# Other places for the steps of two kinds of attention heads in a hand-written instruction order

## The chip, the cores and the metric

The kernel runs on one core of a Trainium2 chip. The time is the device time of one execution in microseconds (us), the median of several runs. A core has a matrix engine (TensorE; PE for its products and PEld for its weight loads in the profile), a vector engine (VectorE, DVE), a scalar engine (ScalarE, ACT), GpSimd (POOL) and SyncE (SP); SP and POOL issue the DMAs here. Each engine works off its own instructions in the order in which the program gives them, and waits on semaphores for the others.

## The reference, cut to what matters

One layer over x (1024 positions by 2048), in fp32. Two groups of eight heads each, of 128 columns, come out of one projection:

```python
hn = rmsnorm(h, norm_mix_g)
sb_q, sb_k, sb_v, sb_g, df_q, df_k, df_v, df_g = split(hn @ w_in)
# stick-breaking heads: weight of key s for query t > s
z = q @ k.T / sqrt(128)
w = exp(log_sigmoid(z[t, s]) - sum(softplus(z[t, j]) for s < j < t))
sb_out = w @ v
# differential heads: two halves of 64 columns, partial rope on q and k
a = softmax(s1) - lam * softmax(s2)            # causal
df_out = rmsnorm(a @ v, subln_g)
mixed = concat(sb_out * silu(sb_g), df_out * silu(df_g))
h = h + mixed @ w_out
h = h + sigmoid(rmsnorm(h) @ w_ple_gate) * (p @ w_ple_proj)
out = rmsnorm(h)
```

## The kernel before, in words

**Arithmetic.** Every fp32 operand of the matrix engine is split into a high and a low part (hi by a cast on ACT, lo by a subtraction on DVE), and a product is three matmuls: hi by hi, hi by lo, lo by hi. So each operand costs ACT a pass and DVE a pass before PE can use it.

**Stages, by the trace.** Up to about 636 us the V and gate columns of the projection are made for all heads and stored (`vg_d`). From there to about 1080 us the heads of the first half of the positions run (`half == 1` in the code, 512 keys), then to about 1640 us those of the second half (`half == 0`, 1024 keys: the new 512 and those of the first half, kept as k_d, kl_d and v_d). The last pair's attention, 1640 to 1766 us, runs beside the first products of the output projection (class `Seven`, operands named A11, A12, S2, S4, S1, S3, A22). Then come the output projection, the gate of the embedding, and the last norm.

**Order of the heads.** `ORDER` alternates a differential head (DF) and a stick-breaking head (SB): a pair. A pair takes 57.4 us in the first half and 74 us in the second.

**The ticks.** `unit` multiplies one head's q and k columns: four chunks of weights, two accumulators (q and k, PSUM tag "acc"), four blocks each, so 32 ticks a head. A tick is three matmuls (L252, L253, L254) and then a call of `side.tick()`. `Side` is a queue of steps with a due tick. A step added with offset t runs floor(t) + 1 ticks later, and among steps of one tick the smaller number goes first; a step with a negative offset runs at once. Offsets are counted from the end of the head's own unit, those of `taken` and of the last pair's operands from the start of one. A step's own parts come by `side.later(dt, ...)`, floor(dt) ticks on (0: in the same tick). The attention of a pair thus lies between the projection matmuls of the heads behind it. The orders of PE, DVE and ACT are the order in which the steps run; those of SP and POOL are made by a scheduler, so a load can go out ahead when its buffer is free. All offsets are in the table `TICK` (L42 to L56).

**The steps.**
- Weights of the projection (`wprep`): raw load, high part on ACT (`whi`, L173), low part on DVE (`wlo`, L169) in the first half; in the second half the low part is loaded back from memory (L175).
- `taken` (L1400, L1404 for SB): the accumulators leave PSUM. For DF (L1426) it goes on by `q_turn` and `k_turn`, seven and eight offsets counted from `taken`: shuffle, product with sine, product with cosine, sum (the rope, four DVE passes, L1452 to L1455); the high parts on ACT (L1432, L1436); the low parts of the two halves on DVE (q L1441, k L1443); and for k the ends, four short casts on ACT (L1450). The store of k for the second half goes out on POOL behind its low parts.
- `scores` (L333 to L336) puts z for one block of 128 rows into one of two z buffers. For SB, `sb_scores` are the offsets of the four row blocks, and `sb_stick` those of the mask (L346), the sigmoids (L359, L360), the scan (L366) and the product (L370) behind it. For DF there are two z per row block; `df_soft` are the offsets, counted from z, of the maximum (`top`, L383), of the exponential (L391, counted from the maximum), of the reciprocal, lambda and scaling (L396 to L398), and of the combination of both softmaxes (L403).
- `values`: V is turned (L418) and split (L420, L423); `sb_v`, `df_v`.
- `turn` (L438): blocks of weights are transposed into PSUM tag "t" (two buffers for turned weights, products and msq); `parts` takes them out: `lead` and `awh` on ACT (L456, L457), `lead` and `awl` on DVE (L461, L462). `mix` (L480 to L485) multiplies by V. `sb_turn` and `df_turn` are the offsets of the second pair of row blocks in each half.
- `sums`: copy (L496) and sum (L499, with a product L501 for SB) of the mixed blocks. `squared` and `norm` for DF: square, product with the gain (L513), split, two matmuls with ones (msq, L530 and L531), two roots on ACT (L534, L535), and four DVE passes (L538 to L541).
- `df_vg`, `sb_vg`: load of V and gate, two products with the norm (L1386), the sigmoid (L1389), the product (L1392).
- Two table loads on ACT per pair (L224 in the profile), for logarithm and exponential (`LOGS`) and for sigmoids (`SIGS`).
- Last pair (`operands`): two offsets for each of the four blocks of an operand, its load (SP) and its split (ACT L627, DVE L633); `wf` the loads of the first output weights, `begun` their splits.

Of the kernel before, what the change touches and what calls it, by code (L numbers as in the profile page):

```python
# [39 lines left out]
GVT = 1, 2, 3, 4, 5, 6, 7, 8, 14, 15, 16, 17  # L40
GLAT = {'S4': 4, 'S1': 4, 'S2': 4}
TICK = {  # L42
    "turn": 76, "lag": 15, "gap": (4, 6), "parts": (1, 2), "vparts": (1, 2), "sums": (1, 2), "squared": (3, 5), "norm": (1, 4),
    "df_scores": (-20, -16, -12, -8, -4, 0, 4, 8), "df_turn": (17, 17), "df_v": -4, "df_norm": 44.5,
    "sb_scores": (-2, 6, 14, 22), "sb_turn": (32, 36), "sb_v": 23,
    "df_soft": (1, 1.5, 4, 5.5), "sb_stick": (1, 1, 3, 5.5), "taken": (28, 31), "sb_split": (1, 2), "kv": 9,
    "df_vg": (24, 36, 37, 57, 58.5), "sb_vg": (6, 17, 18, 26, 27.5),
    "q_turn": (1.5, 5, 7, 8.5, 12, 14, 15.5), "k_turn": (1.5, 13, 14.5, 16, 19.5, 21, 22, 23.5),
# [5 lines left out]
    "begun": (86.5, 92.5, 93.5, 94.5, 92.5),  # L54
}
LAM0 = 0.8 - 0.6 * math.exp(0.0)  # L56
NEG = -1.0e30
# [2274 lines left out]
```

## Time and profile before

| | |
|---|---|
| median of the runs | 2399.39 us (2396.4, 2399.39, 2399.98) |
| the profiled execution | 2398.69 us, its span in the trace 2396.9 us |
| mean granted clock | 0.996 of full speed |
| weights, bytes moved | 359.16 MB read, 203.69 MB written, 235 GB/s |

The span is the time between the first and the last instruction of the trace; the execution's own time is 1.8 us longer. Of the busy shares (the page's first part) it is to be kept in mind that matmuls follow each other before the earlier one has ended, so a busy PE can still lose time between two starts. In lines of the timeline the first number is the start, the second the duration, and the bracket at the end is the idle time of that engine before the instruction, with the one that ended it. In the table of stretches the columns are the busy time and number of instructions of PE, PEld, DVE, ACT and POOL, the granted clock, the DMA's share, and GB/s.

### The profile page before, as it was taken

The numbers are of one execution on the slowest core, as the hardware profiler recorded it, in microseconds if no ns is written. First come the engines' busy times: TensorE is split into PE (matmuls) and PEld (weight loads), VectorE is DVE, ScalarE is ACT, GpSimd is POOL, SyncE is SP. The second block draws the span as 40 slices with busy tenths as digits, with TensorE's granted clock in tenths as the row PEclk, the third lists the DMA queues.
The fourth block names the chain that finished last, engine by engine and source line by source line (L and its number), as shares of the span: only waits on it lengthen the run. The fifth ranks groups of instructions, "written<-read, shape, count | busy, mean of one in ns | idle before, by whom it ended". The sixth has DMA issues, their size and how long they took to land.

```text
span 2396.9 us, 32668 instructions
## 1 busy us (share of the span) xinstructions
PE 2333.0 (97%) x11110; PEld 1934.2 (81%) x11110; DVE 1791.2 (75%) x3115; ACT 1273.9 (53%) x2305; POOL 296.7 (12%) x439
## 2 busy tenths in 40 slices
PE   9999999999999999998999999999899999999998
PEld 7878878888788888877888888887778887888787
DVE  6487786665678888877777777777687987687687
ACT  6323253333366666667666666666542444532455
POOL 2121111111100000000011100110121121111000
PEclk9999999999999999999999999999999999999999
DMA  8587798766787777797667566677787788898965
GB/s 268 203 285 241 252 295 223 178 145 136 223 269 245 236 243 239 252 289 230 196 191 207 171 187 214 181 206 233 219 234 196 251 251 269 303 354 271 316 207 180
DMA packets 255544, 556.66 MB, mean 232 GB/s; under 512 B 28544, under 2 KB 40064, under 8 KB 255376
## 3 DMA queue, kind: packets, MB, share of 16 engines
q1 hardware_dynamic: 186112, 396.18, 50.1%
q0 software_dynamic: 52848, 128.74, 21.8%
q10 hardware_dynamic: 16416, 29.65, 3.4%
q8 instruction: 87, 1.43, 0.2%
q14 instruction: 81, 0.66, 0.1%
HBM read 359.16 MB, written 203.69 MB: 235 GB/s over the span
## 4 chain that ended last, share of the span: by engine, by line
PE 65%; DVE 15%; issue 8%; ACT 7%; DMA 3%; POOL 1%; SPq 0%; ACTq 0%; DVEq 0%; POOLq 0%
PE acc L252 5%; PE acc L254 5%; PE acc L253 5%; PE pbc L650 4%; PE pbc L648 4%; PE pbc L649 4%; PE pc L650 2%; PE pc L649 2%; PE pa L648 2%; PE pc L648 2%; PE pa L650 2%; PE pa L649 2%; DVE z L383 2%; PE pb L1765 2%; PE pb L1764 2%
## 5 line engine op out<-in xcount | busy, mean ns | idle before, releaser
L741 ACT CAST wpr<-T 128x512 fp32r<-128x512 f32 x208 | 127.5, 622 | 479.5 <-DVE T L700 400.1
L252 PE MATMUL acc<-xh,whi 128*128 128x512 f32 x768 | 314.2, 409 | 3.9 <-DVE qk L1404 3.8
L254 PE MATMUL acc<-xh,wlo 128*128 128x512 f32 x768 | 301.6, 393 | 5.1 <-DMA wlo<-wlo_d 4.6
L253 PE MATMUL acc<-xl,whi 128*128 128x512 f32 x768 | 300.8, 392 | 0.0
L254 PEld LDWEIGHTS acc<-xh,wlo 128*128 128x128 f32 x768 | 144.5, 188 | 39.4 <-DMA wlo<-wlo_d 6.3
L252 PEld LDWEIGHTS acc<-xh,whi 128*128 128x128 f32 x768 | 145.3, 189 | 28.8 <-DVE qk L1404 4.3
L253 PEld LDWEIGHTS acc<-xl,whi 128*128 128x128 f32 x768 | 145.2, 189 | 23.7 <-issue 0.2
L173 ACT CAST whi<-wraw 128x1024 fp32r<-128x1024 f32 x128 | 134.4, 1050 | 35.7 <-PE acc L253 20.0
L755 DVE TENSOR_TENSOR wpr<-T,wpr 128x512 fp32r<-128x512 f32 x208 | 142.7, 686 | 8.4 <-ACT wpr L741 5.1
L391 ACT ACTIVATE et<-z,mx 128x512 f32<-128x512 f32 (+7 forms) x128 | 94.8, 741 | 97.5 <-DVE mx L383 97.4
L854 POOL DMA_DIRECT2D vg_d<-hc x128 | 89.2, 697 | 456.3 <-DVE hc L1073 266.6
L741 ACT CAST wpr<-wraw 128x512 fp32r<-128x512 f32 x128 | 79.0, 618 | 114.5 <-DMA wraw<-tw_d 34.6
L457 ACT CAST awh<-tp 128x256 fp32r<-128x256 f32 (+1 forms) x160 | 80.8, 505 | 79.3 <-PE tp L438 79.2
L462 DVE TENSOR_TENSOR awl<-tp,awh 128x256 fp32r<-128x256 f32 (+1 forms) x160 | 92.4, 577 | 31.5 <-ACT awh L457 31.4
L755 DVE TENSOR_TENSOR wpr<-wraw,wpr 128x512 fp32r<-128x512 f32 x128 | 87.0, 686 | 26.5 <-ACT wpr L741 26.2
L383 DVE CUSTOM_DVE_ANT_0 z<-z,wide 128x512 f32<-128x512 f32 (+7 forms) x128 | 97.3, 760 | 5.5 <-PE z L336 4.4
L366 DVE TENSOR_TENSOR_SCAN pt<-pt 128x511 f32<-128x511 f32 (+3 forms) x64 | 86.6, 1354 | 17.2 <-ACT pt L359 16.7
L359 ACT ACTIVATE pt<-z,rcol 128x511 f32<-128x511 f32 (+3 forms) x64 | 47.5, 742 | 73.8 <-DVE z L346 73.6
L169 DVE TENSOR_TENSOR wlo<-wraw,whi 128x1024 fp32r<-128x1024 f32 x56 | 68.5, 1223 | 16.8 <-ACT whi L173 16.1
L485 PE MATMUL av<-awl,v 128*128 128x256 f32 x256 | 74.1, 289 | 3.5 <-DVE awl L462 3.5
L483 PE MATMUL av<-awh,v 128*128 128x256 f32 x256 | 72.0, 281 | 0.2
L484 PE MATMUL av<-awh,v 128*128 128x256 f32 x256 | 72.0, 281 | 0.0
(571 smaller groups left out, 6932.9 us busy)
## 6 DMA issues: line engine op xcount, KB each, us to landing
wraw<-w_in SPq DMA_DIRECT2D x128, 512.0 KB, 4.5
wlo<-wlo_d SPq DMA_DIRECT2D x72, 512.0 KB, 4.2
wraw<-w_vg SPq DMA_DIRECT2D x143, 256.0 KB, 3.6
vg_d<-hc POOLq DMA_DIRECT2D x128, 256.0 KB, 4.9
wlo_d<-wlo SPq DMA_DIRECT2D x56, 512.0 KB, 3.0
wraw<-w_gate SPq DMA_DIRECT2D x92, 256.0 KB, 5.7
h_d<-hc POOLq DMA_DIRECT2D x56, 256.0 KB, 5.2
wraw<-w_out SPq DMA_DIRECT2D x56, 256.0 KB, 4.4
```

Of the source, the lines that this page charges most:

```text
L173: side.later(1, lambda: A.copy(hi[:, o], raw[:, o]))
L252: T.matmul(acc[c], hi[:, k2, kh, c, :], xh, start=first, stop=False)
L253: T.matmul(acc[c], hi[:, k2, kh, c, :], xl, start=False, stop=False)
L254: T.matmul(acc[c], lo[:, k2, kh, c, :], xh, start=False, stop=last)
L383: V.tensor_tensor_reduce(z[:, vw], z[:, vw], add, -DF_SCALE, 3.0e38, ALU.add, ALU.min, mx)
L391: A.activation(et[:, vw], z[:, vw], AF.Exp, bias=mx[:, 0:1], scale=-1.0, accum_out=l[:, c:c + 1])
L462: V.tensor_tensor(wl[:, o, :], tp[:, o, :], wh[:, o, :].bitcast(F32), op=ALU.subtract)
L648: T.matmul(o, wh[:, w], xh, start=start and k == 0, stop=False, skip_group_check=True)
L649: T.matmul(o, wh[:, w], xl, start=False, stop=False, skip_group_check=True)
L650: T.matmul(o, wl[:, w], xh, start=False, stop=k == 3, skip_group_check=True)
L741: A.copy(t[:, 0], src)
L755: V.tensor_tensor(t[:, 1], src, t[:, 0].bitcast(F32), op=ALU.subtract)
```

## The change

Only numbers of `TICK` change; the instructions stay the same, and their order changes.

```diff
-    "sums": (1, 2), "squared": (3, 5),
+    "sums": (0, 2), "squared": (3, 4.5),
-    "df_turn": (17, 17), "df_v": -4,
+    "df_turn": (19, 19), "df_v": -1,
-    "sb_scores": (-2, 6, 14, 22),
+    "sb_scores": (-2, 6, 13.5, 22),
-    "df_soft": (1, 1.5, 4, 5.5),
+    "df_soft": (1.5, 2.0, 4.5, 6.0),
-    "df_vg": (24, 36, 37, 57, 58.5),
+    "df_vg": (25, 37, 41, 58, 59.5),
-    "k_turn": (1.5, 13, 14.5, 16, 19.5, 21, 22, 23.5),
+    "k_turn": (-4.5, 8, 8.5, 10, 13.5, 15, 16, 17.5),
-    "A12": ((17.6, 29), ...
+    "A12": ((18.6, 30), ...
-    "S2": ((28.5, 42), (23.6, 41), (29.5, 59), (29.6, 62)),
+    "S2": ((28.5, 42), (25.6, 43), (33.0, 62), (29.6, 62)),
-    "S4": ((33.5, 62), ...
+    "S4": ((35.5, 64), ...
-    "S1": ((57.5, 70), (58, 73), ...
+    "S1": ((56.5, 70), (58.5, 73), ...
-    "A22": ((87, 101), (88, 104), ...
+    "A22": ((87, 101), (91, 107), ...
-    "begun": (86.5, 92.5, 93.5, 94.5, 92.5),
+    "begun": (86.5, 91.5, 93.5, 94.5, 92.5),
```

In words. For each differential head the shuffle of k runs as soon as k leaves its accumulator (two ticks sooner) and the rest of its rope and split five to six ticks sooner. In its softmax the maximum keeps its tick but stands behind other steps there; the exponential and the combination run a tick later, and the scaling keeps its tick, behind other steps. The turn of the second pair of row blocks comes two ticks later, V's turn three ticks later, and the load and products of V and gate one tick, one product four ticks later. For each stick-breaking head the third row block's scores run a tick sooner. For both kinds the copy of the mixed blocks runs in the tick of the mix itself; for the differential heads the last subtraction of the square runs a tick sooner. In the last pair ten offsets of operands move by one to four ticks (two of them by half a tick to one), and one split of the output weights comes one tick sooner.

More of the change, by code (lines that the diff above doesn't have):

```diff
@@ L42 @@
 TICK = {
[L43 to L48, printed above, removed]
[5 rows of a table removed]
-    "begun": (86.5, 92.5, 93.5, 94.5, 92.5),
+    "turn": 76, "lag": 15, "gap": (4, 6), "parts": (1, 2), "vparts": (1, 2), "sums": (0, 2), "squared": (3, 4.5),
+    "norm": (1, 4), "df_scores": (-20, -16, -12, -8, -4, 0, 4, 8), "df_turn": (19, 19), "df_v": -1, "df_norm": 44.5,
+    "sb_scores": (-2, 6, 13.5, 22), "sb_turn": (32, 36), "sb_v": 23, "df_soft": (1.5, 2.0, 4.5, 6.0),
+    "sb_stick": (1, 1, 3, 5.5), "taken": (28, 31), "sb_split": (1, 2), "kv": 9, "df_vg": (25, 37, 41, 58, 59.5),
+    "sb_vg": (6, 17, 18, 26, 27.5), "q_turn": (1.5, 5, 7, 8.5, 12, 14, 15.5),
[5 rows of a table added]
+    "begun": (86.5, 91.5, 93.5, 94.5, 92.5),
 }
```

10 rows, old and new, of the table TICK are left out of this document.

## Prediction

> **What bounds the kernel now.** I read the page first, then the table of stretches, then the matrix engine's waits stretch by stretch.
>
> ```profile
> span 2396.9 us, 32668 instructions
> ## 1 busy us (share of the span) xinstructions
> PE 2333.0 (97%) x11110; PEld 1934.2 (81%) x11110; DVE 1791.2 (75%) x3115; ACT 1273.9 (53%) x2305; POOL 296.7 (12%) x439
> ```
> ```profile
> 640.00:1019.40 379.40, 374.15 (x1842) 310.61 (x1840) 306.53 (x626) 249.68 (x501) 25.92 (x41) 1.00 0.75 246
> 1156.00:1640.00 484.00, 474.99 (x2536) 400.17 (x2537) 366.94 (x643) 330.93 (x560) 49.55 (x69) 1.00 0.66 194
> ```
>
> PE is the bound everywhere: 374.15 of 379.40 us where the first half's heads run, 474.99 of 484.00 us in the second half. The change takes no matmul away, so all it can win is PE's waits. Here they are in four stretches: first half, passage between the halves, second half, last pair. Columns: who waited for whom, us in total, times, longest.
>
> ```profile
> PE acc L252 <- DVE qk L1404: 2.7, 5, 0.8
> PE acc L254 <- DVE wlo L169: 2.6, 5, 0.5
> ```
> ```profile
> PE acc L254 <- DMA wlo<-wlo_d: 4.6, 3, 2.1
> PE acc L252 <- DVE qk L1404: 4.3, 2, 3.8
> PE tp L438 <- DVE et L403: 1.1, 1, 1.1
> PE z L336 <- DVE kl L1443: 1.0, 1, 1.0
> ```
> ```profile
> PE av L480 <- DVE lead L461: 3.9, 7, 0.6
> PE tp L438 <- DVE et L403: 3.1, 7, 0.5
> PE msq L530 <- DVE awl L462: 1.6, 6, 0.3
> ```
> ```profile
> PE av L480 <- DVE lead L461: 9.0, 3, 4.0
> PE av L485 <- DVE awl L462: 3.5, 5, 1.2
> PE pbc L650 <- DVE wpr L755: 1.4, 1, 1.4
> PE msq L530 <- DVE awl L462: 1.4, 1, 1.4
> PE tp L438 <- DVE et L403: 1.2, 1, 1.2
> ```
>
> The waits come back once per pair of heads, at the same places. PE always waits for DVE, though DVE is busy only 75%: an instruction that is needed stands behind others in DVE's or ACT's order, which TICK fixes. What one wait costs is a little more than its idle time:
>
> ```profile
> 1080.66 0.40 PE L253 MATMUL acc<-xl,whi 128*128 128x512 f32 x1
> 1080.90 0.40 PE L254 MATMUL acc<-xh,wlo 128*128 128x512 f32 x1
> 1085.14 0.80 PE L252 MATMUL acc<-xh,whi 128*128 128x512 f32 x1 [3.84 <-DVE qk L1404]
> ...
> 1088.31 0.40 PE L480 MATMUL av<-lead,v 128*128 128x256 f32 x2
> ```
> ```profile
> 1084.00:1090.00 6.00, 4.86 (x18) 4.17 (x19) 4.69 (x12) 4.20 (x9) 0.68 (x1) 0.72 0.63 186
> 1746.00:1752.00 6.00, 4.21 (x22) 3.38 (x23) 4.17 (x9) 3.97 (x8) 1.17 (x2) 1.00 1.08 231
> ```
>
> A matmul of 512 columns follows the last after 0.24 us (1080.66 to 1080.90), so a tick, three of them, is 0.7 us. From 1080.90 to 1085.14 are 4.24 us, 4.0 too many for a wait shown as 3.84: each wait costs 0.16 us more than its row. After the long wait the granted clock is 0.72 and the eight matmuls from 1085.14 to 1088.31 take 3.17 us in place of at most 1.9: another 1.3 us. In the last row's stretch PE is busy 4.21 of 6.00 us, 1.79 idle, and the clock is 1.00. The Trainium skill, "TensorE: Matmul & The Clock Gate", section "What's actually happening", says that PE falls to half rate after an idle window of some 3.4 us; by it only waits of that length pay this price, and the two rows agree.
>
> **The change part by part.** Every instruction stays; only places in the orders of PE, DVE and ACT move, and with them what their DMAs hang on.
>
> *k's steps, six ticks sooner.* For each differential head, four casts of k (L1432, L1436) and four short casts of its ends (L1450) leave ACT's order between the parts of the stick-breaking head's turns and the roots of the norm; two subtractions (L1443) leave DVE's order there.
>
> ```profile
> 1351.44 1.28 ACT L224 ACT_TABLE_LOAD   x1
> 1352.73 0.59 ACT L457 CAST awh<-tp 128x512 fp32r<-128x512 f32 x1
> 1353.35 1.23 ACT L1450 CAST k<-kl 64x128 fp32r<-64x128 f32 x4
> 1354.60 1.05 ACT L173 CAST whi<-wraw 128x1024 fp32r<-128x1024 f32 x1
> 1355.56 0.68 ACT L534 ACTIVATE avb<-msq,eps 128x512 f32<-128x512 f32 x1
> 1356.27 0.63 ACT L535 ACTIVATE avb<-avb 128x512 f32<-128x512 f32 x1
> ```
> ```profile
> 1356.93 0.69 DVE L538 SCALAR_TENSOR_TENSOR sqv<-msq,avb 128x512 f32<-128x512 f32 x1 [1.69 <-ACT avb L535]
> ...
> 1365.84 0.69 DVE L462 TENSOR_TENSOR awl<-tp,awh 128x512 fp32r<-128x512 f32 x1 [1.75 <-ACT awh L457]
> ```
>
> In the second half the table load starts only after those casts, then awh, the ends (1.23), a weight cast (1.05), and the roots, whose end at 1356.90 starts L538. Without casts and ends in the way the table load goes first and awh waits only for its transposes. So awl comes sooner and msq's wait (0.3 a pair) goes; L538 and all that DVE does behind it start about 1.2 us sooner, the length of the ends. In the first half the table load, too, leaves this path, and I take 1.9 us there.
>
> ```profile
> 844.84 0.63 ACT L284 ACTIVATE neg<-sg 128x512 f32<-128x512 f32 x1 [1.79 <-DVE sg L541]
> ```
> ```profile
> 846.62 0.68 DVE L1404 TENSOR_TENSOR qk<-acc,ssa 128x512 f32<-128x512 f32 x1
> ```
>
> There L1404, which frees the accumulator, ends a chain that starts with L538 (newton steps, neg, q's cast and low part); 1.9 us sooner is more than its wait of 0.5 us, and it goes. In the last pair the casts also clear the way for msq (1.4).
> Against it: the shuffle of k now stands in DVE's order right behind the projection's last matmul and waits there for ACT's copy. Queued behind it are the lead and awl of the differential head's second turn, for which mix waits; but that turn and its mix move two ticks (1.4 us) later as well, more than the shuffle's length (one DVE pass of 512 columns, like L1404's 0.68). I cost it at 0; without that cover it is 0.7 us for each of 16 heads, 11 us. The section "Architectural detail" of the same page says that ACT's and DVE's queues are strictly first in, first out, which is the ground of this price; the 1.75 us above, DVE standing behind one awaited part, agrees.
> The store of k (POOL) is issued six ticks sooner, and in the passage between the halves, where weights already arrive late (4.6 us in three waits), it can push one more: 0 to 2.1 us, the longest of those waits. I take 0, as the loads late there were issued before it. POOL has nothing urgent behind it.
>
> *Softmax a tick later.* exp goes a tick later, the scaling of its row behind the weight cast, and the combination (L403) a tick later.
>
> L403 of row block 1 is what the first turn waits for. By itself the change makes it later by the cast (1.05) and a tick (0.7): 1.75 us. What makes it sooner in the second half: the 1.2 us from L538; the 1.75 us for which DVE stands at 1365.84, since awh and q/k casts now precede the awaited scaling; and 0.7 (a pass of 512 columns) for the gate's product (df_vg 37 to 41), which no longer precedes the maximum. 1.2 + 1.75 + 0.7 - 1.75 = 1.9 us sooner; the wait of 0.5 goes. In the first half L403 also falls behind neg, and I find it about 0.2 us ahead of its need: bounds 0 to 0.5 us of new wait, taken 0.25 for each of 7 heads. The weight's low part (L169) is then ready 2 us ahead, and its wait of 0.5 goes.
>
> *z of row block 2 a tick sooner, second turn two ticks later.*
>
> ```profile
> 1339.42 1.75 DVE L366 TENSOR_TENSOR_SCAN pt<-pt 128x767 f32<-128x767 f32 x1
> 1341.09 0.26 DVE L461 TENSOR_TENSOR lead<-tp,lead 128x128 fp32r<-128x128 f32 x1
> ```
>
> L461 waits for this scan. z now comes before the differential head's last mix (six matmuls, 0.7 us) and a tick sooner: 1.4 us; a sum and a product fall behind L461 and two other passes come ahead of it, each at most a pass of 512 columns (0.7), so I set them against each other. Net about 1.4 us sooner, and the wait of 0.56 goes. What is late next are awl and mix behind it, where DVE does the same fourteen operations as before: 0 to 0.4 us left, taken 0.2 a pair.
>
> *V's turn, gate, sums, squares.* V's turn and its parts run three ticks later and its store on POOL with them; v is first needed five ticks on: 0. load_vg on SP moves a tick, the wide store order stays: 0. The copy for the sums waits on ACT for the mix, at most a tick (0.7), with only the weight cast behind it, which waits for the same chunk: 0, bounds 0 and 0.7 on ACT alone.
>
> *Operands and weights of the last pair.* Their loads (SP) move by one to four ticks, and their casts with them; S2's lie in DVE's way now.
>
> ```profile
> 1698.65 0.69 DVE L633 TENSOR_TENSOR cS2l<-cS2l,cS2h 128x512 fp32r<-128x512 f32 x1 [2.10 <-ACT cS2h L627]
> ```
>
> DVE stands 2.10 us for S2[2] ahead of a scan (L366), and L461, behind both, ends the longest wait, 4.0 us. That operand goes behind the scan, and the mix that waits comes two ticks and one z later (2.8 us): this wait goes, and the drop of the clock after it. The others shrink: I leave 1.5 of the second long wait, 1.0 of the third, 1.4 of L485's 3.5, 0.4 of L438's. A load that lands late instead would cost up to the 2.1 us of a late weight.
>
> **The sum.** First half: 2.7 + 2.6 + 10 times 0.16 = 6.9, less 7 times 0.25: 5.2. Passage: of 4.3 + 1.0 + 1.1 I take away 2.2 of L1404, 1.0 of kl and 1.3 of clock, and add 1.5 at L403, where the exp now stands behind the x casts: 3.0; the DMA waits stay. Second half: 3.9 + 3.1 + 1.6 + 20 times 0.16 = 11.8, less 8 times 0.2: 10.2. Last pair: 9.0 + 3.5 + 1.4 + 1.2 + 10 times 0.16 = 16.7, and 2 drops of the clock, 2.6; less the 4.3 left: 15.0, of which I take 14 for the bounds above. Together 32.4 us of the profiled execution, 2398.69 us (its span and 1.8 us around it): 2366.3. The median of the runs is 0.7 higher: **2367 us**.
>
> **The rivals.**
> *DVE is the next bound (22%).* Fourteen operations follow z of row block 2 without a gap, and I found the mixes behind them met by 0 to 0.4 us only. If awl is 1 us late in each of 8 pairs of the second half, the first half's L403 waits 0.5 more in 7 heads, and the last pair keeps 5 us more: 32.4 - 16.5 = 16 us, 2383. For it: DVE's 306.53 of 379.40 us. Against: 366.94 of 484.00 in the second half.
> *The softmax decides (14%), slower.* Its price is 1.75 us a head at L403, where PE already waits 0.5: 16 heads, 28 us. It decides if L538 is not at least 1 us sooner, for then L1404, L461 and msq keep their waits too and only L169 (3.4) and 10 us of the last pair are won: 28 - 13 = 15 us, 2414. For it: every turn already hangs on L403. Against: L538 visibly starts at the roots' end, behind the ends of k.
> *Nothing moves (6%).* The waits go from one place to the next, within 5 us: 2399.
> The forecast has 58%. All waits touched gone (6.9 + 8.3 + 11.8 + 19.3 = 46 us; 8.3 is the passage's 6.4 with four times 0.16 and the clock's 1.3) would be 2353.
>
> **Range and chances.** 2354 holds nearly all of the best case; 2394 takes in the first rival and reaches to the edge of no change. Outside: slower and most of no change, 18%, and a little at the low end. A measurement of this kernel can tell about 0.2% (5 us). Faster by more 0.80, within 0.06, slower 0.14.
>
> **What would show it.** Right: in the second half no rows of PE behind L461 and msq, and L438 behind L403 gone or under 0.2 a pair; L538 about 1.2 us sooner behind msq; a pair takes about 1.5 us less; no 4 us wait in the last pair. Wrong: L438 behind L403 at 1 us or more a pair, new rows of L485 behind L462 in every pair, or a longer DMA row in the passage.

## The result, and the profile after

The changed kernel took **2359.12 us** in the median (2357.05 to 2364.5) where the kernel before took 2397.89 in the same comparison: a ratio of 0.9842, 95% interval 0.9822 to 0.9862. In a second comparison it took 2363.08 us against 2396.13, ratio 0.9862 (0.9847 to 0.9876). So it is 33 to 39 us faster; 2367 was forecast, in a range of 2354 to 2394. Line numbers of the changed kernel are one lower than before (its table is a line shorter), so L1404 is L1403 there, L403 is L402, and so on.

The page of the changed kernel, and its table of stretches for the inner parts of the two halves (same columns as before):

```profile
span 2362.7 us, 32655 instructions
## 1 busy us (share of the span) xinstructions
PE 2324.6 (98%) x11110; PEld 1937.1 (82%) x11110; DVE 1796.3 (76%) x3115; ACT 1269.2 (54%) x2305; POOL 296.0 (13%) x439
```
```profile
640.00:1010.00 370.00, 370.00 (x1841) 311.37 (x1840) 309.63 (x631) 250.19 (x506) 25.85 (x41) 1.00 0.77 253
1140.00:1600.00 460.00, 456.88 (x2466) 390.05 (x2465) 361.05 (x627) 319.13 (x540) 48.93 (x68) 1.00 0.66 195
```

In the first half PE is now busy 370.00 of 370.00 us: no wait is left. In the second half 3.1 of 460 us are idle, where 9.0 of 484 were. The profiled execution of the changed kernel, 2364.5 us, is the longest of its four, so the two spans differ by 34.2 us and not by the 38.8 of the medians. To see where these 34.2 us lie, one matmul of each pair serves as a milestone: the first one of msq. Its row in the view of that tile gives the number in a window and the first and last start; the fences show the window of the first half and that of the second, for the kernel before and for the changed one.

```profile
L530 PE MATMUL msq<-sqh,onesr x6: 392/398/398, 722.8 to 1010.1; 128*128 128x512 f32 x6
...
L530 PE MATMUL msq<-sqh,onesr x6: 496/496/501, 1206.2 to 1576.0; 128*128 128x512 f32 x6
```
```profile
L529 PE MATMUL msq<-sqh,onesr x6: 398/398/398, 723.1 to 1001.2; 128*128 128x512 f32 x6
...
L529 PE MATMUL msq<-sqh,onesr x6: 398/398/398, 1189.4 to 1550.8; 128*128 128x512 f32 x6
```

Five pairs lie between the first and the last start of a row. A pair in the first half went from 57.46 to 55.62 us, one in the second from 73.96 to 72.28.

| stretch, by these milestones | before | after | gain |
|---|---|---|---|
| five pairs of the first half | 287.3 | 278.1 | 9.2 |
| passage between the halves | 196.1 | 188.2 | 7.9 |
| five pairs of the second half | 369.8 | 361.4 | 8.4 |
| the rest, with the last pair | 820.9 | 811.9 | 9.0 |

(The start lies 0.3 us later.) These stretches are not cut as the prediction's are: the passage here takes in 9 us of its first half and 50 us of its second, the rest 64 us of its second. What PE still waits for, in three windows of the changed kernel: the passage, the second half, and the last pair.

```profile
PE acc L251 <- DVE qk L1403: 3.2, 1, 3.2
PE acc L253 <- DMA wlo<-wlo_d: 0.4, 1, 0.4
```
```profile
PE tp L437 <- DVE avb L498: 1.6, 6, 0.3
PE av L479 <- DVE awl L461: 1.5, 6, 0.3
```
```profile
PE pa L649 <- DMA wflo<-wout_d: 3.2, 1, 3.2
PE av L479 <- DVE awl L461: 1.6, 1, 1.6
PE av L484 <- DVE awl L461: 1.5, 2, 1.3
PE pa L647 <- DMA wfhi<-wout_d: 0.8, 1, 0.8
PE av L479 <- DVE lead L460: 0.4, 1, 0.4
```

The rows of L1404 and L169 are gone from the first half; those of L403, of lead and of msq from the second, where two short ones (0.26 and 0.27 us) stand in their place; the last pair's 9.0 us behind lead have become 0.4, but a new wait for the output projection's weights has come up, 3.2 and 0.8 us.

### The profile page after: what moved, and what is told of

It is laid out like the page before. It is cut to its first block, busy times and chain, and to the rows that moved or that the text cites. A ratio compares the mean times of both kernels' runs of the same rounds, so it can differ in the third digit from the quotient of the medians.

```text
span 2362.7 us, 32655 instructions
## 1 busy us (share of the span) xinstructions
PE 2324.6 (98%) x11110; PEld 1937.1 (82%) x11110; DVE 1796.3 (76%) x3115; ACT 1269.2 (54%) x2305; POOL 296.0 (13%) x439
```

## The experiments

The theory is that of the prediction: k's casts and ends stood in ACT's order ahead of the roots, and everything DVE does behind the roots came late. The rivals were that the moves help each by itself or only as a whole, that the softmax's new place decides, and that DVE is the next bound. All twelve runs in one table: medians, ratio to the kernel before in the same comparison, and the stretches as above, from the msq rows and the span of one profiled execution of each kernel. That of the old softmax is the shortest of its four, 2354.37 us beside 2362.69 to 2365.13, so its rest is not to be compared with the others.

| run | us | ratio (95%) | pair, first half | passage | pair, second half | rest |
|---|---|---|---|---|---|---|
| k alone | 2379.05 | 0.9930 (0.9915 to 0.9945) | 55.54 | 188.9 | 73.40 | 824.1 |
| all but k | 2391.93 | 0.9981 (0.9972 to 0.9990) | 58.84 | 194.0 | 73.42 | 814.4 |
| old softmax | 2363.67 | 0.9868 (0.9852 to 0.9885) | 55.54 | 187.5 | 72.30 | 805.1 |
| softmax alone | 2396.16 | 0.9996 (0.9986 to 1.0005) | 58.22 | 193.0 | 73.10 | 822.5 |
| old turn | 2374.36 | 0.9908 (0.9893 to 0.9923) | 55.62 | 188.4 | 72.86 | 817.7 |
| k and turn alone | 2365.98 | 0.9878 (0.9862 to 0.9895) | 55.50 | 190.3 | 72.80 | 809.1 |
| old operands | 2361.11 | 0.9846 (0.9832 to 0.9861) | 55.62 | 188.2 | 72.28 | 806.9 |
| weights sooner | 2363.58 | 0.9861 (0.9844 to 0.9877) | 55.60 | 187.8 | 72.30 | 815.1 |
| scan first | 2378.08 | 0.9920 (0.9903 to 0.9936) | 55.60 | 195.2 | 73.22 | 813.5 |
| sum and scan | 2373.61 | 0.9900 (0.9882 to 0.9919) | 55.56 | 189.5 | 73.20 | 816.3 |
| before again | 2397.24 | one run | 57.40 | 194.0 | 73.90 | 822.5 |
| changed again | 2363.08 | 0.9862 (0.9847 to 0.9876) | 55.62 | 187.8 | 72.28 | 811.7 |

### k alone, and all but k

```diff
-    "k_turn": (1.5, 13, 14.5, 16, 19.5, 21, 22, 23.5),
+    "k_turn": (-4.5, 8, 8.5, 10, 13.5, 15, 16, 17.5),
```

Made in the kernel before:

> The kernel before with k_turn alone moved. Theory (k's casts and ends stood ahead of the roots on ACT): the first half's waits for L1404 and L169 go (a pair 57.4 to about 55.6 us, 10 us in all), the second half loses the waits at L403, msq and behind the newton steps (1.3 us a pair, 10 us) and keeps the 0.7 us behind lead; the passage loses the 4 us behind L1404: about 2375. Rival (the shuffle, now ahead of the second turn's lead and awl, costs 0.7 us a head while that turn stays where it was): only the first half and the passage gain, the second half keeps its 74 us a pair or more: 2387 or above.

And undone in the changed kernel:

> The changed kernel with k_turn back in its old place. Theory (the other moves put L403 1.75 us later and only k's steps pay for that): every first turn waits for L403 more than a microsecond longer, the first half's waits for L1404 return, 2405 to 2415, slower than before. Rival (the moves help each by itself, so what k's steps bring is just missing): 2370 to 2385.

Measured: 2379.05 (17 us of the gain) and 2391.93 (5 us of it). k alone clears the first half completely: its pair falls to 55.54 us. The path is the forecast one: with k alone L538 follows msq after 2.47 us in the first half (832.28 to 834.75) and after 2.05 in the second, and with all but k after 4.59 (841.23 to 845.82) and 2.83, as before. In the second half k alone takes away the waits behind msq and most of those behind L403 but doubles the ones behind lead. The waits of PE there, k alone:

```profile
PE av L480 <- DVE lead L461: 7.0, 12, 0.7
PE tp L438 <- DVE et L403: 1.2, 6, 0.2
```

All but k, its waits in the first half:

```profile
PE tp L437 <- DVE et L402: 4.6, 5, 0.9
PE z L335 <- DVE kl L1442: 4.3, 5, 0.9
PE acc L251 <- DVE qk L1403: 3.4, 5, 0.7
```

Without k's move the later softmax and the other moves cost the first half 1.4 us a pair (58.84); with it they cost nothing. In the profiled executions the whole brings 34.2 us and the two parts 18.0 and 3.6; of the 12.6 us between, 6.5 lie in the five pairs of the first half (a gain of 9.2 against one of 9.6 and a loss of 6.9) and 5.7 in the rest. The theory's 2375 for k alone holds within 4 us, but partly by luck: the passage gained 7.2 us where 4 were expected, a pair of the second half 0.56 where 1.3 were, since the rival's price, 0.7 us behind lead, is there as well, and the rest is 3.2 us longer. Without k the kernel isn't slower than before, as the theory had it (2405 to 2415), nor as fast as the rival had it (2370 to 2385).

### Old softmax, and softmax alone

```diff
-    "df_soft": (1.5, 2.0, 4.5, 6.0),
+    "df_soft": (1, 1.5, 4, 5.5),
```

> The changed kernel with df_soft back at (1, 1.5, 4, 5.5). Theory (a later exp and combination let the weight's cast and low part go first): the first half's wait for L169 returns, 0.9 us a pair, and little else: 2364 to 2370. Rival A (the later softmax buys nothing, or costs): 2350 to 2359. Rival B (the later softmax carries the second half as well): a pair there above 73.5 us, 2375 or more.

The other way round, the new df_soft alone in the kernel before:

> The kernel before with df_soft alone at (1.5, 2, 4.5, 6). Theory (as in the prediction's second rival, its price is the cast and a tick at L403, 1.75 us, in both halves): L438 waits 2 us or more behind L403 in every pair, 2415 to 2428. Rival (the price is under 1 us and only in the first half, since in the second half L403 is held by the exponentials' own row and not by the scaling): 2398 to 2408, the first half's pair about 58.5 us and the second half's about 74.

With the old softmax the pairs take 55.54 and 72.30 us, as in the changed kernel, and L169's wait doesn't return. By the pairs that is rival A: the later softmax buys nothing there beside the other moves. The median, 2363.67 us, lies between the ranges of the theory (2364 to 2370) and of rival A (2350 to 2359), and these runs can't tell it from the changed kernel's 2359.12 and 2363.08. Alone the later softmax is no change in the whole (2396.16), which neither the theory (2415 to 2428) nor the rival (2398 to 2408) had, by opposite effects: in the first half L438 waits 1.4 us a pair behind L403 while L169's wait goes (a pair 58.22), in the second L438's wait is gone but for one of 0.6 us (73.10 in place of 73.96). Three rows of DVE's timeline there, softmax alone:

```profile
1355.25 0.69 DVE L538 SCALAR_TENSOR_TENSOR sqv<-msq,avb 128x512 f32<-128x512 f32 x1 [1.68 <-ACT avb L535]
...
1362.53 0.69 DVE L462 TENSOR_TENSOR awl<-tp,awh 128x512 fp32r<-128x512 f32 x1
...
1365.05 1.28 DVE L403 SCALAR_TENSOR_TENSOR et<-et,l 128x1024 f32<-128x1024 f32 x1 [0.16 <-ACT et L398]
```

DVE still stands 1.68 us ahead of L538: the roots are as late as before. But L462, at which it stood 1.75 us before, now starts without a wait, since awh goes ahead of the scaling on ACT. So in the second half the new order of the softmax pays for its own delay, and the price of 1.75 us a head does not exist there.

### Old turn, and k and turn alone

```diff
-    "df_turn": (19, 19),
+    "df_turn": (17, 17),
-    "sb_scores": (-2, 6, 13.5, 22),
+    "sb_scores": (-2, 6, 14, 22),
```

> The changed kernel with df_turn back at (17, 17) and the third row block's scores back at 14. Theory (the two moves remove the wait behind lead and nothing else): about 0.9 us a pair returns in the second half, 7 us, and two of the long waits in the last pair, 5 to 8 us: 2371 to 2376. Rival (k's shuffle now delays lead as well, so the old places are worse than they were): 1.6 us or more a pair in both halves, 2385 or more.

It cost 11 to 15 us against the two comparisons of the changed kernel: nothing in the first half, 0.58 a pair in the second, and 6 us in the rest, where the longest wait behind lead is 3.6 us again. The theory's range holds; and the rival's mechanism is there too, without its size. PE waits behind lead twice a pair now (6.3 us in 12 waits), and the DVE timeline at the second place shows what stands ahead of it:

```profile
1306.20 0.73 DVE L1451 STREAM_SHUFFLE sw<-qk 128x512 f32<-128x512 f32 x1
1306.83 0.01 DVE L1451 LOAD_MASK_SELECT sw<-qk  x1
1306.83 0.76 DVE L1451 STREAM_SHUFFLE sw<-qk 128x512 f32<-128x512 f32 x1
1307.49 0.27 DVE L460 TENSOR_TENSOR lead<-tp,lead 128x128 fp32r<-128x128 f32 x1
```

The shuffle is two passes, 1.3 us from 1306.20 to 1307.49, and not the one pass of 0.7 us that the prediction took; PE waits 0.5 us behind it. The two ticks of the later turn, 1.4 us, cover even that.

The other direction, k's steps with these two entries alone in the kernel before:

> The kernel before with k_turn, df_turn and the third row block's scores (13.5) alone. Theory (these two parts carry the change; softmax, V's turn, gate, sums, squares and operands bring nothing beside them): the second half's pair at 72.3 us, the first half's at 55.6 us, in all 2356 to 2366. Rival (the smaller moves are needed to keep DVE's order clear once the two are made): a pair in the second half at 73 us or more, 2368 or above.

2365.98 us, at the edge of the theory's 2366: nearly the whole gain. The pair of the second half, 72.80, lies between the two cases. Its waits there:

```profile
...
PE tp L438 <- DVE et L403: 1.4, 6, 0.5
```

Ahead of this row stand the two short waits of the changed kernel, 1.6 us each. This one is missing there, and with the old softmax too (72.30); so beside k and turn the moves of V's turn, gate, sums and squares are enough to remove it. Which of them, was not separated, and the later softmax, which all but removed it by itself above, may be enough as well.

### Old operands, and weights sooner

The last pair's entries back in the changed kernel (the minus lines of the change for A12, S2, S4, S1, A22 and begun, twelve offsets of operands and one of weights):

> The changed kernel with the last pair's operands (A12, S2, S4, S1, A22) and begun back in their old places. Theory (S2's split ahead of the scan made the 4 us wait of the last pair): 4 us of waits behind lead and awl return in the last pair and nothing changes elsewhere: 2362 to 2367. Rival (the later second turn alone removed that wait): 2356 to 2361, the last pair as in the changed kernel.

2361.11 us: no difference to the changed kernel (2359.12 and 2363.08) that these runs resolve, and a time between the theory's range and the rival's. But the last pair is not the same. Its waits with the old operands:

```profile
PE av L479 <- DVE lead L460: 3.1, 2, 2.4
...
PE tp L437 <- DVE et L402: 1.3, 1, 1.3
...
PE pa L649 <- DMA wflo<-wout_d: 0.6, 1, 0.6
```

2.7 us behind lead and 1.3 behind L402 return, and the 3.2 and 0.8 us behind the weights shrink to 0.6. So the moved operands do take their waits away, but a load of the output projection's weights is then late. The reason lies more in the load than in PE: the low part that PE waits for is issued at 1647.29 us in the changed kernel and lands 12.1 us later, where with the old operands it takes 9.9 us from its issue at 1645.48; PE comes to it 8.8 us after the issue in the one (1656.05, behind its wait of 0.8 us for the high part) and 9.1 in the other (1654.59). Why the load takes longer was not tried. In the profiles the rest is even 5 us shorter with the old operands (806.9 against 811.9), and the granted clock from 1640 to 1770 us is 1.00 against 0.97. Of the 4.0 us behind lead, the second turn's move alone leaves 2.4 (here) and the operands' alone 3.6 (old turn): both are needed.

Are the late weights chance?

> The changed kernel, unchanged, in other executions. Theory (late weights of the output projection in the last pair differ between executions): its waits behind wfhi and wflo differ from the 4.0 us of the first profile by more than 1 us and the total with them, while the pair in the second half stays at 72.3 us. Rival (the late weights belong to its order): 3.5 to 4.5 us again, and a span within 2 us of 2362.7.

The same waits came again (wflo 3.1, wfhi 0.8 us; a span of 2360.4), so they belong to this order; the rival holds, but for a span 2.3 us shorter where it allowed 2. Every other profile with the moved operands shows 3.1 to 4.6 us behind wflo, only the old softmax's 0.7, in the shortest execution of its kernel; every profile with the old operands shows 0.9 or none.

```diff
-    "wf": (21.5, 25, 33, 45, 49, 61, 66, 77),
+    "wf": (21.5, 25, 33, 41, 45, 61, 66, 77),
```

> The changed kernel with the loads of the output weights 3 and 4 (wf) at 41 and 45, four ticks sooner. Theory (PE now reaches the fifth weights sooner than their loads, which are issued behind the fourth's and behind stores on SP, can land): issued sooner, they land sooner, the 3.9 us behind wfhi and wflo shrink to under 2 and the drop of the clock goes: 2354 to 2358. Rival (their issue waits for a buffer that the products hold, whatever the tick): the same 3 to 4 us and 2359 to 2364.

2363.58 us, with 3.1 and 1.9 us behind the weights: nothing won, as the rival had it. The expectation speaks of the fifth weights; by the trace it is the fourth for which PE waits (the load issued at 1647.29 lands at 1659.4, when the wait ends), and the edit moves both. The fourth's low part is issued where it was (SP's timeline, changed kernel, then this run):

```profile
1647.29 0.50 SPq L1323 DMA_DIRECT2D wflo<-wout_d  x1
```
```profile
1646.12 0.51 SPq L1323 DMA_DIRECT2D wflo<-wout_d  x1
```

1.2 us sooner, as the whole execution is at that point (its last msq at 1549.6, 1.2 us ahead): the tick doesn't set its issue. That a buffer does was argued, not tried.

### Before again

The kernel before, unchanged:

> The kernel before, unchanged, in another execution. Theory (how late the weights land in the passage between the halves is chance of the execution): the rows of PE behind the loaded low part there differ from the 4.6 us of three waits by more than 1.5 us, while the waits behind L403, L404's neighbours L1404, L461 and L462 come back to 0.2 us. Rival (they belong to the order of the kernel): 4 to 5 us again in the same three places, and the change removed them.

The waits of DVE's and ACT's order came back in the halves and the last pair to 0.4 us; in the passage that of 1.1 us behind L403 is gone and the one behind kl is 1.9 us in place of 1.0. Of the late weights in the passage only part did:

```profile
PE acc L254 <- DMA wlo<-wlo_d: 2.2, 2, 1.5
```

2.2 us in place of 4.6. So a part of the passage's 7.9 us is a matter of the execution: against this one the passage gains 5.8.

### Two attempts to go further

The two short waits left in each pair of the second half stand behind a scan that waits for the sigmoids, which wait behind q's four casts on ACT, and behind a sum that stands behind q's second low part on DVE.

```diff
-    "q_turn": (1.5, 5, 7, 8.5, 12, 14, 15.5), "x0": (5, 6, 13, 14),
+    "q_turn": (1.5, 5, 7, 8.5, 12.5, 16.2, 16.6), "x0": (5, 6, 16, 17),
-    "A11": ((8.5, 13), (8.6, 15), (9.5, 21), (9.6, 23)),
+    "A11": ((8.5, 17), (8.6, 19.5), (9.5, 21), (9.6, 23)),
-    "S4": ((35.5, 64), (38.5, 70), (42.5, 73), (45.5, 75)),
+    "S4": ((35.5, 64), (38.5, 70), (42.5, 75.5), (45.5, 75)),
-    "S1": ((56.5, 70), (58.5, 73), (58.5, 76), (75.5, 85)),
+    "S1": ((56.5, 70), (58.5, 75.6), (58.5, 76), (75.5, 85)),
```

> The changed kernel with q_turn (1.5, 5, 7, 8.5, 12.5, 16.2, 16.6), so that the sigmoids of the third row block go ahead of q's four casts on ACT and the sum ahead of q's two low parts on DVE; x0 (5, 6, 16, 17), and S4[2] 75.5, S1[1] 75.6, A11 17 and 19.5 for the splits that DVE has ahead of a scan or of awl in the last pair. Theory (what is left is again order ahead of the scan and ahead of L1403): the two waits of 0.26 us a pair in the second half go (0.85 us a pair), the passage's 3.2 us behind L1403 falls under 2, and the last pair's 1.3 and 1.6 us shrink: 2345 to 2352. Rival (DVE is now the bound, so each place given up makes the next one late): the waits come back at msq or at awl of the second turn, 2356 to 2364.

```diff
-    "sums": (0, 2), "sb_scores": (-2, 6, 13.5, 22), "q_turn": (1.5, 5, 7, 8.5, 12, 14, 15.5),
+    "sums": (0, 1), "sb_scores": (-2, 6, 12.5, 22), "q_turn": (1.5, 5, 7, 8.5, 12, 14.9, 15.5),
```

> The changed kernel with sums (0, 1), the third row block's scores at 12.5 and q_turn's first low part at 14.9. Theory (the scan of that block stands behind q's four casts, and the sum behind q's second low part): both waits of 0.26 us go without a new one, a pair in the second half at 71.4 us, 2350 to 2356. Rival (the copy and the mix now make DVE wait for the sum, and something else comes late by as much): 72.3 us or more a pair, 2358 or above.

Both are slower than the changed kernel, 2378.08 and 2373.61 us, with 73.2 us a pair. The waits of "scan first" in the second half:

```profile
PE av L484 <- DVE awl L461: 5.9, 6, 1.0
PE av L479 <- ACT k L1431: 2.1, 5, 0.4
```

The stall that was aimed at shrinks, and another comes behind it: DVE stood 1.38 us ahead of the scan in the changed kernel and now stands 0.38, but then 1.77 us for awh ahead of lead, and the awl of the next turn comes 1.0 us late.

```profile
1324.46 1.75 DVE L365 TENSOR_TENSOR_SCAN pt<-pt 128x767 f32<-128x767 f32 x1 [0.38 <-ACT pt L358]
1327.98 0.29 DVE L460 TENSOR_TENSOR lead<-tp,lead 128x128 fp32r<-128x128 f32 x1 [1.77 <-ACT awh L456]
```

The same edit moved the casts of x in the passage later, and the profile shows 3.9 us there behind L402 (a passage of 195.2 in place of 188.2). What the rivals had holds in both, a step given a later place delays the next matmul; only that "scan first" is 14 us above the rival's range. Other orders of this place were not tried. No version here beats the changed kernel by more than these runs resolve.

## Why the prediction was right, point by point

**The bound, and k's steps: right; the time in the second half too large.** The forecast was that L538 comes 1.2 us sooner behind msq in the second half and 1.9 in the first. Before, msq to L538, first half (PE, then DVE):

```profile
837.53 0.40 PE L530 MATMUL msq<-sqh,onesr 128*128 128x512 f32 x1
```
```profile
841.93 0.69 DVE L538 SCALAR_TENSOR_TENSOR sqv<-msq,avb 128x512 f32<-128x512 f32 x1
```

After:

```profile
834.41 0.40 PE L529 MATMUL msq<-sqh,onesr 128*128 128x512 f32 x1
```
```profile
836.69 0.69 DVE L537 SCALAR_TENSOR_TENSOR sqv<-msq,avb 128x512 f32<-128x512 f32 x1
```

4.40 us became 2.28: 2.1 sooner, where 1.9 were forecast. In the second half 2.83 us (1354.10 to 1356.93) became 2.06 (1333.89 to 1335.95), 0.8 sooner and not 1.2: the roots are now ready too early and wait for msq itself.

```profile
1334.56 0.69 ACT L533 ACTIVATE avb<-msq,eps 128x512 f32<-128x512 f32 x1 [1.17 <-PE msq L530]
```

Only with msq's own delay, which is gone (0.27 us of its row and the 0.16 of the forecast), is it 1.2. k alone shows that this carries the first half by itself.

**The first half's size: too small.** The waits of the forecast lie in five pairs, those between the milestones: 5.2 us were expected there, and 9.2 gained. Two terms were off. The new wait of 0.25 us behind L403 never came. And a wait costs more than its row and 0.16 us. Before, at L1404's wait:

```profile
846.48 0.39 PE L254 MATMUL acc<-cA11h,wlo 128*128 128x512 f32 x1
847.36 0.50 PE L252 MATMUL acc<-cA11h,whi 128*128 128x512 f32 x1 [0.50 <-DVE qk L1404]
847.70 0.40 PE L253 MATMUL acc<-cA11l,whi 128*128 128x512 f32 x1
```

From 846.48 to 847.70 are 1.22 us where two steps of 0.23 would be: 0.76 for a row of 0.50, since the matmul behind the wait delays the next as well. Two such waits a pair are 1.5 of the 1.84 us; the rest was not followed up.

**The passage: more than twice what was expected.** Taken at 3.0 us, it gained 7.9; without the two thirds of a pair of the second half that the stretch takes in, some 6.8. The prediction let the three waits for loaded low parts stay (4.6 us); 0.4 is left. They are partly chance (2.2 in the other execution of the same kernel), and in no run with a changed order did they exceed 2.1. What moved them was not found. Of the long wait behind L1404 less went than taken: 3.8 became 3.2 us, and the clock drops after it still, for longer (0.51 from 1069 to 1075 us of the changed kernel), so the 1.3 us taken for it were not won. The 1.5 us added at L403 did not come either, and its 1.1 went. The stretch as a whole goes by k's steps: 187.5 to 190.3 us in every kernel that has them sooner, but for "scan first", and 193.0 to 196.1 in every one that has not.

**The softmax: no gain and no price.** The net of 1.9 us sooner at L403 is right as far as its wait is gone; its size was not measured. But the step adds nothing beside the others (old softmax), and the second rival's price of 1.75 us a head was wrong: alone the step costs 0.8 us a pair in the first half and nothing in the second. The stall of 1.75 us at L462 that was to pay for it was read correctly; it pays even without k.

**z of row block 2 and the second turn: right, and the second half right in sum by luck.** The wait behind lead is gone; with the old places it is back, and with it the shuffle's price that the two ticks were to cover. That price was mis-sized, 0.7 us for each of 16 heads: the shuffle is twice as long, but the old places cost 0.58 a pair in the second half alone. The 10.2 us of the second half lie in 484 us, 6.5 pairs, so 1.56 a pair; 1.68 was measured. Two errors cancel in it. What is late next was put at 0.2 us a pair; the two waits of 0.26 and 0.27 with what they add come to 0.84 of PE's time (from 1320.63 to 1321.27 and from 1321.82 to 1322.37, where steps of 0.23 and 0.12 would be). And the removed waits had cost more than their rows and 0.16 each, as in the first half.

**The last pair: half of what was expected.** 14 us were taken there; all behind the last milestone, most of a pair of the second half included, is 9.0. The operands' step failed: they bring nothing that these runs can measure. Their waits go, and late weights take their place, 4.0 us. "A load that lands late instead" was in the prediction as a cost of up to 2.1 us, and taken at almost nothing. Nor did the drops of the clock go that were taken at 2.6: before, it was 0.79 from 1704 to 1712 us and 0.72 from 1724 to 1730, and in the changed kernel it is 0.72 from 1658 to 1664 and from 1692 to 1698.

So the total, 32 us expected and 33 to 39 measured, is right by the mechanism of its main step, but its closeness is luck: the first half and the passage brought some 4 us more each than they were taken at, the last pair 6 to 7 less.

## What to carry to other kernels

Where engines work in program order, look for the instruction whose finish many others stand behind (here the roots on ACT) and ask what is ahead of it that nobody needs yet; moving that is worth more than every other step together, and the other moves may cost something without it. A wait of 0.50 us cost PE half as much again as its row says. And an order that takes an engine's waits away can make a load land later: of a wait removed beside large transfers, count only what they allow.

## What the runs showed of the hardware

The clock drops after shorter waits than expected. The prediction took 1.3 us for each wait of about 4 us, with a stretch of 1.79 us idle at full clock as the other case. In the changed kernel's last pair PE waits 1.65 us, and from 1693.8 us on its matmuls follow each other after 0.43 us in place of 0.23:

```profile
1692.33 0.48 PE L479 MATMUL av<-lead,v 128*128 128x256 f32 x2 [1.65 <-DVE awl L461]
```

What decides is shown by stretches of the length of a drop, 3.41 us. In this kernel the drops of the last pair begin at 1659.67 and 1693.80 us, ten such lengths apart; here are the stretches just before and in each of them, and the one behind the second:

```profile
1656.26:1659.67 3.41, 0.23 (x1) 0.23 (x2) 0.06 (x1) 0.00 (x0) 0.00 (x0) 1.00 1.10 262
1659.67:1663.08 3.41, 3.41 (x15) 3.10 (x15) 1.18 (x3) 0.00 (x0) 0.00 (x0) 0.50 1.06 364
...
1690.39:1693.80 3.41, 1.53 (x12) 1.09 (x10) 3.41 (x7) 0.81 (x2) 0.84 (x1) 1.00 1.10 339
1693.80:1697.21 3.41, 3.41 (x11) 2.73 (x9) 2.18 (x4) 1.86 (x4) 0.85 (x1) 0.50 0.02 3
1697.21:1700.62 3.41, 3.41 (x22) 3.02 (x22) 1.00 (x3) 1.24 (x2) 0.00 (x0) 1.00 0.79 139
```

The clock is exactly halved for 3.41 us after a stretch in which PE idled 1.88 us of 3.41. In the kernel before, the 1.79 us that left the clock at 1.00 are spread over three stretches of the same grid; the two with most idle time have 1.54 and 0.84 us:

```profile
1743.42:1746.83 3.41, 1.87 (x9) 1.19 (x7) 2.66 (x6) 0.85 (x2) 3.17 (x4) 1.00 0.71 116
1746.83:1750.24 3.41, 2.57 (x16) 2.33 (x17) 2.75 (x6) 1.38 (x4) 0.00 (x0) 1.00 1.08 249
```

Laid out like this from the drops of each of the fourteen profiles, 54 drops begin at full clock between 700 and 2340 us, and each follows a stretch with at least 1.71 us idle, half of it; only three stretches with that much idle time are followed by none (1.76, 1.82 and 1.89 us). So it is the idle time within a fixed stretch of 3.41 us that counts, whether in one wait or in several, and about half of it is enough. The Trainium skill, "TensorE: Matmul & The Clock Gate", section "What's actually happening", puts the threshold at an idle window of some 3.4 us; the length agrees with these traces, but the window need not be idle throughout. Where a wait falls on this grid is then chance: the one behind L1403 in the passage was 2.58 us in the old softmax's profile, fell into two stretches (1.50 and 1.08 us idle) and left the clock at 1.00, and 2.55 us in that of "weights sooner", fell into one and halved it. The executions of the changed kernel in the first comparison differ along with it: 2357.05, 2358.02, 2360.23 and 2364.5 us at a mean granted clock of 0.998, 0.997, 0.996 and 0.995.
